# Scan outputs of two head groups per visit to TensorE's column halves, broadcast rows in one run, and two prices in the planner

## The chip, the cores and the metric

The kernel runs on one core of one Trainium2 chip. The metric is the device time of one execution in microseconds (us), the median of several runs. TensorE is PE in the profile (its weight loads are PEld), VectorE is DVE, ScalarE is ACT, GpSimd is POOL, and SP is the engine whose queue issues almost all transfers.

## The reference, cut to what matters

One layer of a hybrid model works on 128 prompt tokens and 2048 latent tokens. Eight heads of differential attention and sixteen heads of a two-directional state-space scan share one input projection and one output projection. The scan runs in 17 chunks of 128 tokens. For each chunk and head, the part that the change touches is

```
seg    = a_cum[q] - a_cum[s]
Lmat   = exp(where(mask, seg, -inf))
cb     = C[q] . B[s]                       # shared by the 4 heads of a group
y_diag = (cb * Lmat) @ (x * dt)            # 128 x 128 by 128 x 64 for each head
y_off  = (C @ h_prev) * exp(a_cum)         # h_prev: state at the chunk's edge, 64 x 64
y      = y_diag + y_off                    # both directions are summed
```

The sixteen heads lie in four groups (g) of four heads. The prompt chunk (chunk 0) starts from a state of zero and has no `y_off`.

## The kernel before, in words

The whole program is recorded first and ordered afterwards. `body` calls operations on a `Plan`; each call becomes an `Op` with a price (`price`), the operations that it depends on, and a function that emits the real instruction. `latest` walks the recorded order backwards and gives each operation a due time, with TensorE's operations due in the order in which they were recorded. `simulate` then plays the program forward on the prices, one operation per engine at a time, and among those that are ready takes the one that is due first. A DMA occupies a modelled wire for its price. What comes out is the order of every engine's queue and of SP's DMA queue; on the chip each queue runs strictly in that order. All instructions are emitted by one helper, so that the profile shows one line (L233) for all of them.

The change is in the stage of the scan outputs (`ssd_outputs`). It runs beside the projection units of q, k, g and z: `run_units` puts one or two steps of the scan (`pipe(k)`) between the matmuls of a projection unit (24 matmuls in three products of hi and lo parts, PSUM tile `ps_p`) and that unit's eviction. `G` lists the 68 pairs of chunk and head group, from chunk 16 down to chunk 0. For pair j:

- `loads(j)`, at step j, issues the transfers on SP's queue. `ar` receives the decay rows of a group, two directions by four heads by 128 tokens, broadcast to all 128 partitions from `row_d` (512 KB written). For g = 0 it also loads `bz`, `cd`, `hb` (the states, from `hb_d`) and `xs`.
- `stage_a1(j)`, at step j + 2: ACT takes exponentials of the rows into `ea` and DVE multiplies them by `cd`; POOL masks `ar`, ACT takes eight more exponentials, and PE forms `ps_cb` (fp32, 128 columns of weights). For g = 0 DVE first updates `hb` by way of `hd`, and so waits for the load of `hb`.
- `stage_a2(j)`, the same step: DVE adds the two directions into `ms` and multiplies by `ps_cb`.
- `stage_m(j)`, at step j + 3: PE forms the outputs of four heads. Each matmul has 64 columns of weights and writes one half of the PSUM partitions, so two heads run side by side in the column halves of the array. For two pairs of heads and two terms (`xs` by `ms`, then `hb` by `ea`) these are eight matmuls in fp32, each of which the trace shows as two records: 16 records on `ps_y`. Chunk 0 has the first term only, 8 records.
- `stage_e(j)`: ACT copies `ps_y` (128x256) to `y`, and a DMA stores it to `y_d`.

`ms` has two buffers, `ea` and `ar` three, the PSUM tag `y` two banks. The rows in `row_d` are written by `dt_rows`, earlier, from transposes of `a_all`, in the order chunk, direction, head, token: the four heads of a group are 2 KB in one run, and a group's two directions lie 8 KB apart.

In `price` a DMA costs by its innermost run, up to 4096 bytes; for the broadcast of `ar` that is 256 runs of 2 KB, 1.35 us of the modelled wire. A matmul with 64 columns of weights has a price of its own, but going from full columns to column halves and back costs nothing in `simulate`.

Of the kernel before, what the change touches and what calls it, by code (L numbers as in the profile page):

```python
# [18 lines left out]
P = 128  # L19
# [148 lines left out]
class Op:  # L168
    __slots__ = ("i", "eng", "emit", "cost", "deps", "weak", "outs", "then", "n", "late", "due", "start", "end", "tab", "port")

# [25 lines left out]
class Plan:  # L196


    def __init__(self, tc):
        self.tc, self.ops, self.last, self.floor, self.line, self.lean = tc, [], None, None, None, False  # L200
        for k in ("tensor", "vector", "scalar", "gpsimd", "sync"):
            setattr(self, k, Engine(self, k))
# [13 lines left out]
    def add(self, eng, name, args, kw):  # L216
# [13 lines left out]
        def emit():  # L230
# [3 lines left out]

        op = Op(i, eng, emit, self.price(eng, name, named))
        f = str(named.get("func", "")).rsplit(".", 1)[-1]
        op.tab = TABLE.get(f)
        inside = sum(isinstance(v, View) and not v.t.pool.psum and math.prod(v.shape[1:]) > 1
                     for k, v in named.items() if k not in ("out", "accum_out"))
# [4 lines left out]
        if self.line is not None and eng == "dma":  # L244
            op.weak.update(self.line)
            self.line[:] = [i]
        self.ops.append(op)
        for v in reads + writes:
# [17 lines left out]
        op.weak.discard(i)  # L266
        op.weak -= op.deps

    def touch(self, op, v, write):
# [20 lines left out]
    def price(self, eng, name, a):  # L290
# [3 lines left out]
        if eng == "dma":  # L294
            named_in = a["in_"]
            run = min(4096, 4 * min(o.shape[-1], named_in.shape[-1]))
            return max(math.prod(o.shape) * 4 / run * max(9.7 + 0.0365 * run, 28.4) / 16, 180.0) if run > 4 else 180.0
        n = max([size(o)] + [size(v) for v in ins[:1]])
# [72 lines left out]
    def simulate(self):  # L371
# [4 lines left out]
        free = dict.fromkeys(ENG, 0.0)  # L376
        wire, table, port = 0.0, None, 0.0
        pend = {e: [] for e in ENG}
# [28 lines left out]
        while True:  # L407
# [21 lines left out]
            if be == "dma":  # L429
                wire = max(wire, bt + 700) + op.cost  # L430
                end = wire + 1100
                free[be] = max(bt + 480, wire - 1500)
            else:
                c = op.cost
                if op.tab and op.tab != table:
                    c += 1283
                    table = op.tab
                if op.port:
                    c += max(port - bt, 0.0)
                    port = bt + c  # L440
                free[be] = end = bt + c
# [6 lines left out]
def body(tc, I, O):  # L448
# [17 lines left out]
    xt_d = dp.tile([NCH, P, D], F32, name="xt_d")  # L466
    row_d = dp.tile([NCH, 2, 16, P], F32, name="row_d")
    hb_d = dp.tile([NCH, P, D], F32, name="hb_d")
# [481 lines left out]
    def dt_chain():  # L950
        t_a, t_b, t_c = (vc.tile([P, NCH, 32], F32, name=n, tag=n) for n in ("t_a", "t_b", "t_c"))
        dts["t"] = (t_a, t_b)
        nc.vector.tensor_scalar(out=t_a, in0=dt_all, scalar1=-1.0, scalar2=None, op0=ALU.mult)
# [15 lines left out]
    def dt_sums():  # L969
        t_a, t_b = dts["t"]  # L970
        for d, tri in enumerate((triu, tril)):
            sl = slice(d * 16, d * 16 + 16)
            pc = bank("tr")
            mm(pc[:, :272], lhsT=tri, rhs=t_a[:, :, sl], start=True, stop=True)
            nc.vector.tensor_copy(out=a_all[:, :, sl], in_=pc[:, :272].rearrange("p (c h) -> p c h", h=16))
            po = bank("y")
            mm(po[:, :272], lhsT=ones, rhs=t_a[:, :, sl], start=True, stop=True)
            nc.vector.tensor_copy(out=t_b[:, :, sl], in_=po[:, :272].rearrange("p (c h) -> p c h", h=16))
        nc.scalar.activation(out=dec_all, in_=t_b, func=AF.Exp)
        nc.vector.tensor_tensor(out=t_b, in0=t_b, in1=a_all, op=ALU.subtract)  # L980
        nc.scalar.activation(out=t_b, in_=t_b, func=AF.Exp)
        nc.vector.tensor_tensor(out=w_all, in0=t_b, in1=dt_all, op=ALU.mult)
        nc.vector.tensor_scalar(out=dt_all, in0=dt_all, scalar1=TINY, scalar2=None, op0=ALU.max)
        nc.scalar.activation(out=dt_all, in_=dt_all, func=AF.Ln)
        nc.vector.tensor_tensor(out=dt_all, in0=dt_all, in1=a_all, op=ALU.subtract)

    def dt_rows(c0):
        k = min(4, NCH - c0)
        pr = bank("tr")
        for i in range(k):  # L990
            nc.tensor.transpose(pr[:32, i * P:(i + 1) * P], a_all[:, c0 + i, :], ident)
        rw = vc.tile([32, 512], F32, tag="rw", name="rw", bufs=2)
        nc.vector.tensor_copy(out=rw[:, :k * P], in_=pr[:32, :k * P])
        store(out=row_d[c0:c0 + k].rearrange("c d h t -> (d h) c t"),
              in_=rw[:, :k * P].rearrange("r (c t) -> r c t", t=P))
# [106 lines left out]
    def ssd_outputs(sp):  # L1102
# [9 lines left out]
        def loads(j):  # L1112
# [3 lines left out]
            if g == 0:  # L1116
# [9 lines left out]
                if c:  # L1126
# [4 lines left out]
            ar = sp.tile([P, 2, 4, P], F32, tag="ar", name="ar", bufs=3)  # L1131
            load(out=ar.rearrange("p d h t -> p d (h t)"),
                 in_=row_d[c, :, g * 4:g * 4 + 4, :].rearrange("d h t -> d (h t)").unsqueeze(0).to_broadcast(
                     [P, 2, 512]))
            w[0], w[1] = ar[:, 0], ar[:, 1]

        def stage_a1(j):
# [8 lines left out]
            if c:  # L1146
                ea = w["es"] = sp.tile([P, 4, P], F32, tag="ea", name="ea", bufs=3)
                nc.scalar.activation(out=ea[0:64], in_=w[0][0:64], func=AF.Exp)
# [12 lines left out]
        def stage_a2(j):  # L1161
            w = W[j]
            ms = w["ms"] = sp.tile([P, 4, P], F32, tag="ms", name="ms", bufs=2)
            nc.vector.tensor_tensor(out=ms, in0=w[0], in1=w[1], op=ALU.add)
# [3 lines left out]
        def stage_m(j):  # L1168

            c, g = G[j]  # L1170
            w, k = W[j], CK[c]
            py = w["py"] = bank("y")
            for i in range(2):
                o = py[:, i * P:(i + 1) * P]
                for n, (st, mv) in enumerate((("xs", "ms"), ("hb", "es"))[:2 if c else 1]):
                    for e in range(2):
                        cs = slice((g * 4 + 2 * i + e) * 64, (g * 4 + 2 * i + e + 1) * 64)
                        mm(o[e * 64:e * 64 + 64], lhsT=k[st][:, cs], rhs=w[mv][:, 2 * i + e],
                           start=n == 0, stop=n == 1 or not c)

        def stage_e(j):
            c, g = G[j]
            w = W.pop(j)
            y = sp.tile([P, 2, P], F32, tag="y", name="y", bufs=2)
            nc.scalar.copy(out=y, in_=w["py"][:, :256].rearrange("p (i t) -> p i t", t=P))
            store(out=y_d[2 * g:2 * g + 2, :, c * P:(c + 1) * P].rearrange("i p t -> p i t"), in_=y)

        def pipe(k):
            n = len(G)
            if k == 0:  # L1190
                init()
            if 0 <= k - 3 < n:
                stage_m(k - 3)
            if 0 <= k - 2 < n:
                stage_a1(k - 2)
            if 0 <= k - 3 < n:
                stage_e(k - 3)
# [651 lines left out]
```

## Time and profile before

| what | value |
|---|---|
| median of 3 runs | 3131.48 us (3130.55 to 3132.58) |
| the profiled execution, its own time | 3144.34 us |
| its span, first to last instruction | 3142.6 us |
| mean granted TensorE clock | 0.992 |
| PE busy over the span | 3073.5 us (98%) |
| chain that ended last, share of PE | 78%; DMA 10%, DVE 8% |

The page's second part cuts the span into 40 slices; PE is at nine tenths or more in all but the first. The stage of the scan outputs lies from about 846 to 1432 us. A record's duration is not the time that it costs, since matmuls are pipelined: what an instruction costs PE is read from the distance between starts. An engine's "idle before" names what ended the wait, which may be an engine or a transfer.

### The profile page before, as it was taken

How to read it: one execution, taken by the hardware profiler on the slowest of the kernel's cores; microseconds unless marked ns; L12 is line 12 of the kernel's file. 1: busy time of each engine (PE TensorE's matmuls, PEld its weight loads, DVE VectorE, ACT ScalarE, POOL GpSimd, SP SyncE). 2: the span in 40 equal slices, each digit the busy share in tenths (PEclk: the TensorE clock that was granted, in tenths of full speed). 3: DMA queues.
4: the chain of work that ended last, by engine and by line, in shares of the span. 5: the costliest groups of instructions: out<-in, count | busy, mean ns of one | idle time of the engine just before them, and what ended most of it. 6: DMA issues, size and time to landing. Idle time of an engine off the chain costs nothing.

```text
span 3142.6 us, 56037 instructions
## 1 busy us (share of the span) xinstructions
PE 3073.5 (98%) x20539; PEld 2900.9 (92%) x20539; DVE 2309.5 (73%) x4636; ACT 1835.9 (58%) x3290; POOL 1327.3 (42%) x1171
## 2 busy tenths in 40 slices
PE   7999999999999999999999999999999999999999
PEld 5999999988999998898999999999999999878887
DVE  5544524767675776664699999999999999877775
ACT  3233312333465676663588888888888888754432
POOL 2010100000021122220499999999999999800000
PEclk9999999999999999999999999999999999999999
DMA  8633322677788788879313131222222221296663
GB/s 282 214 120 102 125 80 96 200 234 227 215 254 238 224 228 210 224 198 224 89 41 95 35 96 50 80 67 68 65 67 65 66 64 46 82 275 195 182 189 106
DMA packets 490725, 449.27 MB, mean 143 GB/s; under 512 B 34991, under 2 KB 437704, under 8 KB 490450
## 3 DMA queue, kind: packets, MB, share of 16 engines
q1 hardware_dynamic: 488530, 445.52, 48.8%
q8 instruction: 162, 2.65, 0.4%
q14 instruction: 113, 0.93, 0.1%
q10 hardware_dynamic: 1920, 0.17, 0.0%
HBM read 305.96 MB, written 139.62 MB: 142 GB/s over the span
## 4 chain that ended last, share of the span: by engine, by line
PE 78%; DMA 10%; DVE 8%; issue 2%; SPq 1%; ACT 1%; POOL 0%; DVEq 0%; POOLq 0%; ACTq 0%
PE ps_p L233 28%; PE ps_s L233 17%; PE ps_o L233 13%; PE ps_t L233 8%; PE ps_v L233 4%; PE ps_y L233 3%; PE ps_f L233 3%; DMA yL<-y_d 2%; SPq L233 1%; DVE o L233 1%; DVE yx L233 1%; PE ps_tr L233 1%; PE ps_cb L233 1%; DMA hb<-hb_d 1%; DMA vr<-in_w_in 1%
## 5 line engine op out<-in xcount | busy, mean ns | idle before, releaser
L233 DVE TENSOR_SCALAR_CACHE_REDUCE S<-ps_s 128x768 f32<-128x768 f32 x768 | 726.4, 953 | 65.3 <-PE ps_s L233 50.3
L233 POOL TENSOR_TENSOR S<-S,S 128x768 f32<-128x768 f32 x384 | 708.0, 1866 | 5.0
L233 PE MATMUL ps_s<-K,q 128*128 128x384 f32 x3072 | 707.6, 348 | 0.4 <-DVE S L233 0.3
L233 PE MATMUL ps_p<-hH,wH 128*128 128x384 f32 (+1 forms) x2112 | 699.6, 331 | 0.0
L233 PE MATMUL ps_p<-hH,wL 128*128 128x384 f32 (+1 forms) x2112 | 691.4, 327 | 0.4 <-DVE wL L233 0.4
L233 PE MATMUL ps_p<-hL,wH 128*128 128x384 f32 (+1 forms) x2112 | 691.4, 327 | 0.0
L233 ACT ACTIVATE S<-S,mx 128x2304 f32<-128x2304 f32 x256 | 570.9, 2230 | 12.9 <-DVE mx L233 12.9
L233 PEld LDWEIGHTS ps_s<-K,q 128*128 128x128 f32 x3072 | 505.8, 189 | 2.6 <-DVE S L233 2.1
L233 PE MATMUL ps_o<-aH,V 128*128 128x256 f32 x2304 | 490.9, 286 | 0.0
L233 POOL TENSOR_SCALAR_AFFINE_SELECT ar<-ar 128x512 f32<-128x512 f32 x136 | 113.4, 839 | 746.9 <-ACT ea L233 686.6
L233 ACT CAST aH<-ps_t 128x384 fp32r<-128x384 f32 x768 | 347.7, 481 | 133.5 <-PE ps_t L233 130.1
L233 DVE TENSOR_TENSOR aL<-ps_t,aH 128x384 fp32r<-128x384 f32 x768 | 406.1, 550 | 25.7 <-ACT aH L233 21.7
L233 PEld LDWEIGHTS ps_p<-hH,wL 128*128 128x128 f32 x2112 | 399.2, 189 | 1.7 <-DVE wL L233 1.1
L233 PEld LDWEIGHTS ps_p<-hH,wH 128*128 128x128 f32 x2112 | 399.6, 189 | 1.1 <-issue 0.6
L233 PEld LDWEIGHTS ps_p<-hL,wH 128*128 128x128 f32 x2112 | 399.9, 189 | 0.4 <-issue 0.2
L233 POOL TENSOR_SCALAR S<-S,sm 128x768 f32<-128x768 f32 x384 | 346.4, 916 | 91.9 <-DVE sm L233 82.0
L233 PEld LDWEIGHTS ps_o<-aH,V 128*128 128x128 f32 x2304 | 380.9, 189 | 0.1
L233 PE MATMUL ps_t<-cst,S 128*128 128x128 f32 x2304 | 355.9, 272 | 1.3 <-DVE aL L233 1.3
L233 PE MATMUL ps_o<-aL,V 128*128 128x256 f32 x1152 | 330.0, 286 | 0.0
L233 PEld LDWEIGHTS ps_t<-cst,S 128*128 128x128 f32 x2304 | 285.3, 140 | 16.4 <-DVE aL L233 1.5
L233 DVE TENSOR_TENSOR wL<-wr,wH 128x1024 fp32r<-128x1024 f32 x88 | 110.9, 1260 | 191.8 <-ACT wH L233 188.5
L233 PEld LDWEIGHTS ps_o<-aL,V 128*128 128x128 f32 x1152 | 218.2, 189 | 0.5 <-DVE mx L233 0.3
(245 smaller groups left out, 4737.0 us busy)
## 6 DMA issues: line engine op xcount, KB each, us to landing
wr<-in_w_in SPq DMA_DIRECT2D x88, 512.0 KB
ar<-row_d SPq DMA_DIRECT2D x68, 512.0 KB
q<-qH_d SPq DMA_DIRECT2D x128, 128.0 KB
q<-qL_d SPq DMA_DIRECT2D x128, 128.0 KB
xb<-xbc_d SPq DMA_DIRECT2D x17, 640.0 KB
K<-kH_d SPq DMA_DIRECT2D x48, 192.0 KB
K<-kL_d SPq DMA_DIRECT2D x48, 192.0 KB
V<-vH_d SPq DMA_DIRECT2D x24, 384.0 KB
```

Of the source, the lines that this page charges most:

```text
L233: getattr(e, name)(*[rl(v) for v in args], **{k: rl(v) for k, v in kw.items()})
```

## The change

1. `stage_m` is called for every second pair and covers two head groups: it forms the outputs of pairs j - 1 and j in one PSUM bank (four blocks of 128 columns in place of two). The new `Plan.together` records all its matmuls as one operation, so that they stay in one piece. `pipe` calls `stage_m` and `stage_e` at even steps only. `stage_e` copies 128x512 at once and stores four rows of tiles in one DMA. `ms` gets four buffers and `ea` five.
2. `row_d` is laid out by chunk, group, direction, head, token, so that a group's rows are one run of 4 KB; the broadcast reads `[P, 1024]` from one run. For this `dt_sums` makes two more DVE copies (into `t_c`, in the new order), and `dt_rows` transposes `t_c`.
3. The planner charges 95 ns whenever TensorE goes between matmuls with 64 columns of weights and anything else, and prices a broadcast of `row_d` at 300 ns for each 4 KB over 16 engines, 2.4 us.

```diff
+        if self.one:
+            op = self.ops[self.one[0]]
+            op.emit = lambda a=op.emit: (a(), emit())
+            op.cost += self.price(eng, name, named)
+            i = op.i
+        else:
+            op = Op(i, eng, emit, self.price(eng, name, named))
+            self.ops.append(op)
+        if self.one is not None:
+            self.one[:] = [i]
...
+        op.half = name == "matmul" and named["lhsT"].shape[-1] == 64
...
+    def together(self, f):
+
+        self.one = []
+        f()
+        self.one = None
...
+            if isinstance(named_in, View) and named_in.t.kw["name"] == "row_d":
+                return math.prod(o.shape) * 4 / 4096 * 300.0 / 16
...
+                if be == "tensor" and op.half != half:
+                    c += 95
+                    half = op.half
...
-    row_d = dp.tile([NCH, 2, 16, P], F32, name="row_d")
+    row_d = dp.tile([NCH, 4, 8 * P], F32, name="row_d")
...
+            nc.vector.tensor_copy(out=t_c.rearrange("p c (g d h) -> p c g d h", g=4, d=2)[:, :, :, d],
+                                  in_=a_all[:, :, sl].rearrange("p c (g h) -> p c g h", g=4))
...
-            nc.tensor.transpose(pr[:32, i * P:(i + 1) * P], a_all[:, c0 + i, :], ident)
+            nc.tensor.transpose(pr[:32, i * P:(i + 1) * P], t_c[:, c0 + i, :], ident)
...
-            load(out=ar.rearrange("p d h t -> p d (h t)"),
-                 in_=row_d[c, :, g * 4:g * 4 + 4, :].rearrange("d h t -> d (h t)").unsqueeze(0).to_broadcast(
-                     [P, 2, 512]))
+            load(out=ar.rearrange("p d h t -> p (d h t)"), in_=row_d[c, g].unsqueeze(0).to_broadcast([P, 1024]))
...
-                ea = w["es"] = sp.tile([P, 4, P], F32, tag="ea", name="ea", bufs=3)
+                ea = w["es"] = sp.tile([P, 4, P], F32, tag="ea", name="ea", bufs=5)
...
-            ms = w["ms"] = sp.tile([P, 4, P], F32, tag="ms", name="ms", bufs=2)
+            ms = w["ms"] = sp.tile([P, 4, P], F32, tag="ms", name="ms", bufs=4)
...
         def stage_m(j):
 
-            c, g = G[j]
-            w, k = W[j], CK[c]
-            py = w["py"] = bank("y")
-            for i in range(2):
-                o = py[:, i * P:(i + 1) * P]
-                for n, (st, mv) in enumerate((("xs", "ms"), ("hb", "es"))[:2 if c else 1]):
-                    for e in range(2):
-                        cs = slice((g * 4 + 2 * i + e) * 64, (g * 4 + 2 * i + e + 1) * 64)
-                        mm(o[e * 64:e * 64 + 64], lhsT=k[st][:, cs], rhs=w[mv][:, 2 * i + e],
-                           start=n == 0, stop=n == 1 or not c)
+            py = W[j]["py"] = bank("y")
+
+            def run():
+                for j2 in (j - 1, j):
+                    c, g = G[j2]
+                    w, k = W[j2], CK[c]
+                    for i in range(2):
+                        o = py[:, (g % 2 * 2 + i) * P:(g % 2 * 2 + i + 1) * P]
+                        for n, (st, mv) in enumerate((("xs", "ms"), ("hb", "es"))[:2 if c else 1]):
+                            for e in range(2):
+                                cs = slice((g * 4 + 2 * i + e) * 64, (g * 4 + 2 * i + e + 1) * 64)
+                                mm(o[e * 64:e * 64 + 64], lhsT=k[st][:, cs], rhs=w[mv][:, 2 * i + e],
+                                   start=n == 0, stop=n == 1 or not c)
+            pl.together(run)
 
         def stage_e(j):
             c, g = G[j]
+            del W[j - 1]
             w = W.pop(j)
-            y = sp.tile([P, 2, P], F32, tag="y", name="y", bufs=2)
-            nc.scalar.copy(out=y, in_=w["py"][:, :256].rearrange("p (i t) -> p i t", t=P))
-            store(out=y_d[2 * g:2 * g + 2, :, c * P:(c + 1) * P].rearrange("i p t -> p i t"), in_=y)
+            y = sp.tile([P, 4, P], F32, tag="y", name="y", bufs=2)
+            nc.scalar.copy(out=y, in_=w["py"].rearrange("p (i t) -> p i t", t=P))
+            store(out=y_d[2 * g - 2:2 * g + 2, :, c * P:(c + 1) * P].rearrange("i p t -> p i t"), in_=y)
 
         def pipe(k):
             n = len(G)
             if k == 0:
                 init()
-            if 0 <= k - 3 < n:
+            full = 0 <= k - 3 < n and k % 2 == 0
+            if full:
                 stage_m(k - 3)
             if 0 <= k - 2 < n:
                 stage_a1(k - 2)
-            if 0 <= k - 3 < n:
+            if full:
                 stage_e(k - 3)
             if 0 <= k - 2 < n:
                 stage_a2(k - 2)
```

## Rows read from the trace of the kernel before

**Rows 1.** The page, its first part: busy time of each engine, its share of the span and its instructions.

```profile
PE 3073.5 (98%) x20539; PEld 2900.9 (92%) x20539; DVE 2309.5 (73%) x4636; ACT 1835.9 (58%) x3290; POOL 1327.3 (42%) x1171
```

**Rows 2.** Stretches of the span, for the stage of the scan outputs (from the first broadcast to the last visit). Columns: the stretch, its length, busy us (and instructions) of PE, PEld, DVE, ACT and POOL, then the granted TensorE clock as a share of full speed, the busy share of the 16 DMA engines, and GB/s.

```profile
846.00:1432.00 586.00, 573.02 (x4008) 543.45 (x4007) 405.55 (x710) 370.59 (x926) 113.42 (x136) 0.99 0.81 223
```

**Rows 3.** Instructions of PE in order of time around one full visit to the column halves. Columns: start, duration, engine, line, operation and tiles, shape, and how many were merged into the row.

```profile
871.12 0.33 PE L233 MATMUL ps_p<-hL,wH 128*128 128x384 f32 x1
871.30 0.34 PE L233 MATMUL ps_p<-hH,wL 128*128 128x384 f32 x1
871.57 0.44 PE L233 MATMUL ps_y<-ms,xs 128*64 128x128 f32 x4
871.84 0.39 PE L233 MATMUL ps_y<-ea,hb 128*64 128x128 f32 x4
872.05 0.39 PE L233 MATMUL ps_y<-ms,xs 128*64 128x128 f32 x4
872.27 0.39 PE L233 MATMUL ps_y<-ea,hb 128*64 128x128 f32 x4
872.59 0.49 PE L233 MATMUL ps_cb<-cd,bz 128*128 128x128 f32 x2
872.83 0.42 PE L233 MATMUL ps_p<-hH,wH 128*128 128x384 f32 x1
873.09 0.33 PE L233 MATMUL ps_p<-hL,wH 128*128 128x384 f32 x1
```

**Rows 4.** The same view around the last visit of the stage. It belongs to chunk 0, which has no state term, so it holds half as many matmuls, and a projection follows it directly.

```profile
1430.09 0.34 PE L233 MATMUL ps_p<-hH,wL 128*128 128x384 f32 x1
1430.36 0.66 PE L233 MATMUL ps_y<-ms,xs 128*64 128x128 f32 x8
1430.95 0.44 PE L233 MATMUL ps_p<-hH,wH 128*128 128x384 f32 x1
1431.23 0.34 PE L233 MATMUL ps_p<-hL,wH 128*128 128x384 f32 x1
```

**Rows 5.** The same view around a product of B and C (`ps_cb`) that stands alone among projections, with no visit ahead of it.

```profile
864.04 0.34 PE L233 MATMUL ps_p<-hH,wL 128*128 128x384 f32 x1
864.21 0.38 PE L233 MATMUL ps_cb<-cd,bz 128*128 128x128 f32 x2
864.35 0.36 PE L233 MATMUL ps_p<-hH,wH 128*128 128x256 f32 x1
864.55 0.28 PE L233 MATMUL ps_p<-hL,wH 128*128 128x256 f32 x1
864.67 0.28 PE L233 MATMUL ps_p<-hH,wL 128*128 128x256 f32 x1
```

**Rows 6.** The instructions that read or write the PSUM tile `ps_y`: counts, and durations in ns (minimum/median/maximum), first and last start in us.

```profile
L233 PE MATMUL ps_y<-ms,xs x544: 272/273/421, 871.6 to 1430.7; 128*64 128x128 f32 x182
L233 ACT COPY y<-ps_y x68: 345/373/380, 876.0 to 1431.2; 128x256 f32<-128x256 f32 x68
L233 ACT COPY s_b<-ps_y x36: 579/581/584, 642.5 to 842.1; 64x512 f32<-64x512 f32 x36
```

**Rows 7.** Who waited for whom in the stretch 846 to 1440 us, on PE, DVE and the DMA queue of SP: total us, times, longest.

```profile
PE ps_tr L233 <- DVE kl L233: 8.5, 2, 7.1
PE ps_y L233 <- DVE ms L233: 4.1, 1, 4.1
DVE hb L233 <- DMA hb<-hb_d: 46.8, 10, 11.7
SPq L233 <- DMA ar<-row_d: 19.4, 17, 3.1
```

**Rows 8.** Instructions in order of time on the DMA queue of SP and on DVE ahead of the two longest stalls of the stage. In brackets: idle time of the engine before the instruction, and what ended it.

```profile
1212.00 0.38 SPq L233 DMA_DIRECT2D z_d<-so  x1
1215.58 0.37 SPq L233 DMA_DIRECT2D y_d<-y  x1
1216.04 0.42 SPq L233 DMA_DIRECT2D ar<-row_d  x1
1216.55 0.46 SPq L233 DMA_DIRECT2D hb<-hb_d  x1
1224.72 1.22 DVE L233 TENSOR_TENSOR hb<-hb,hd 64x1024 f32<-64x1024 f32 x1 [7.89 <-DMA hb<-hb_d]
1323.35 1.22 DVE L233 TENSOR_TENSOR hb<-hb,hd 64x1024 f32<-64x1024 f32 x1 [11.70 <-DMA hb<-hb_d]
```

**Rows 9.** Stretches as in rows 2: the two stalls of PE, each with the stretch behind it.

```profile
1220.40:1227.50 7.10, 0.04 (x1) 0.00 (x0) 2.71 (x3) 0.00 (x0) 0.00 (x0) 0.76 0.60 202
1227.50:1231.00 3.50, 3.42 (x12) 3.42 (x13) 3.47 (x11) 3.34 (x10) 1.27 (x2) 0.52 0.46 105
1321.80:1326.00 4.20, 0.14 (x1) 0.00 (x0) 2.62 (x4) 0.00 (x0) 0.00 (x0) 1.00 0.27 96
1326.00:1330.00 4.00, 3.96 (x25) 3.66 (x26) 3.66 (x9) 2.03 (x6) 0.70 (x2) 0.57 0.71 127
```

**Rows 10.** Stretches as in rows 2: first one in which almost only a broadcast of `row_d` into `ar` is under way (two runs of 2 KB for each of 128 partitions), then one with a broadcast of `rs_d` into `rb` alone (one run of 4 KB for each of 128 partitions, the same 512 KB; output projection).

```profile
976.70:980.60 3.90, 3.90 (x29) 3.73 (x26) 3.80 (x7) 2.26 (x4) 0.64 (x1) 1.00 0.81 169
2849.50:2851.60 2.10, 2.10 (x11) 1.74 (x10) 2.10 (x4) 0.72 (x2) 0.00 (x0) 1.00 0.80 244
```

**Rows 11.** One instruction of DVE in order of time: a copy of 128x272 out of PSUM in `dt_sums`.

```profile
603.84 0.42 DVE L233 COPY t_b<-ps_y 128x272 f32<-128x272 f32 x1
```

More of the change, by code (lines that the diff above doesn't have):

```diff
@@ L168 @@
 class Op:
-    __slots__ = ("i", "eng", "emit", "cost", "deps", "weak", "outs", "then", "n", "late", "due", "start", "end", "tab", "port")
+    __slots__ = ("i", "eng", "emit", "cost", "deps", "weak", "outs", "then", "n", "late", "due", "start", "end", "tab", "port", "half")
     def __init__(self, i, eng, emit, cost):
@@ L199, in __init__ @@
     def __init__(self, tc):
-        self.tc, self.ops, self.last, self.floor, self.line, self.lean = tc, [], None, None, None, False
+        self.tc, self.ops, self.last, self.floor, self.line, self.lean, self.one = tc, [], None, None, None, False, None
         for k in ("tensor", "vector", "scalar", "gpsimd", "sync"):
@@ L246, in add @@
             self.line[:] = [i]
-        self.ops.append(op)
         for v in reads + writes:
@@ L376, in simulate @@
         free = dict.fromkeys(ENG, 0.0)
-        wire, table, port = 0.0, None, 0.0
+        wire, table, port, half = 0.0, None, 0.0, False
         pend = {e: [] for e in ENG}
@@ L951, in dt_chain @@
         t_a, t_b, t_c = (vc.tile([P, NCH, 32], F32, name=n, tag=n) for n in ("t_a", "t_b", "t_c"))
-        dts["t"] = (t_a, t_b)
+        dts["t"] = (t_a, t_b, t_c)
         nc.vector.tensor_scalar(out=t_a, in0=dt_all, scalar1=-1.0, scalar2=None, op0=ALU.mult)
@@ L969, in dt_sums @@
     def dt_sums():
-        t_a, t_b = dts["t"]
+        t_a, t_b, t_c = dts["t"]
         for d, tri in enumerate((triu, tril)):
@@ L987, in dt_rows @@
     def dt_rows(c0):
+        t_c = dts["t"][2]
         k = min(4, NCH - c0)
@@ L990, in dt_rows @@
         for i in range(k):
-            nc.tensor.transpose(pr[:32, i * P:(i + 1) * P], a_all[:, c0 + i, :], ident)
+            nc.tensor.transpose(pr[:32, i * P:(i + 1) * P], t_c[:, c0 + i, :], ident)
         rw = vc.tile([32, 512], F32, tag="rw", name="rw", bufs=2)
         nc.vector.tensor_copy(out=rw[:, :k * P], in_=pr[:32, :k * P])
-        store(out=row_d[c0:c0 + k].rearrange("c d h t -> (d h) c t"),
+        store(out=row_d[c0:c0 + k].rearrange("c g (e t) -> (g e) c t", t=P),
               in_=rw[:, :k * P].rearrange("r (c t) -> r c t", t=P))
```

1 line of the change is left out of this document (removed).

## The prediction

> **What bounds the kernel now.** I read the busy parts of the page first: PE is busy for 98% of the span, the next engine, DVE, for 73% [rows 1]. Then the stretch of the scan outputs alone: of 586 us PE is busy 573, DVE 406, ACT 371, POOL 113, and the 16 DMA engines 81% [rows 2]. So in this stage, too, PE sets the end, DMA is the one resource that comes near, and DVE, ACT and POOL have a third of their time free. Two things shorten it: fewer nanoseconds of PE per visit, and fewer stalls. Work that only leaves ACT, DVE or SP's queue is worth nothing by itself. Idle PE is 13 us of the 586; the list of waits puts 8.5 us on DVE's `kl` and 4.1 us on DVE's `ms` [rows 7].
>
> **What a visit costs, and what the change removes.** Durations of PE's records overlap, so I use distances between starts. In the visit at 871.57 us, from the last projection matmul before it (871.30) to the second one after it (873.09) pass 1.79 us [rows 3]. What should that stretch hold at a steady rate? A projection matmul of 384 columns takes 0.17 (from 864.04 to 864.21 [rows 5]; from 871.12 to 871.30 in the rounded rows of [rows 3]). A block of four `ps_y` records inside the visit takes 0.43 / 2 = 0.215 (871.84 to 872.27 [rows 3]); there are four. For the two records of `ps_cb`, the one that stands alone gives 864.04 to 864.55 = 0.51 for itself, a 384-column and a 256-column matmul; less 0.17 and 0.12 (864.55 to 864.67) that is 0.22 [rows 5]. Sum: 0.17 + 4 x 0.215 + 0.22 + 0.17 = 1.42. The excess is 0.37 us.
>
> Is the excess per visit, or per matmul? The visit at 1430.36 has 8 records and no `ps_cb` behind it: 1430.09 to 1431.23 = 1.14 us against 0.17 + 2 x 0.215 + 0.17 = 0.77, an excess of 0.37 again [rows 4]. So it comes once per visit, whether it is long or short and whatever follows. It lies at the edges: about 0.1 between the last full matmul and the first half one, the slow first block (0.27 to the next block instead of 0.215), about 0.1 on the way out, and about 0.1 in the first full weights after it. The trace shows 544 `ms` records, 8 for each of 68 visits, and 68 copies of `ps_y` [rows 6]. The change makes 34 visits, by construction: the recorded unit can't be torn apart. 34 x 0.36 (a little under the excess, for rounded starts) = 12.2 us, all on PE's path. The bounds are 10 (0.30, if part of the edge is a wait that a longer visit keeps) and 13.
>
> Which steps could take some of that back? The 34 `ps_cb` that no longer follow a visit stand alone, and a lone one costs no more than its own work [rows 5]: nothing. The matmuls themselves are the same in number and shape.
>
> **What leaves the other engines.** 68 ACT copies of 368 to 373 ns become 34 of 128x512, for which the copies of 64x512 out of the same tile, 581 ns, are the nearest row [rows 6]: 25.4 - 19.8 = 5.6 us of ACT that is not the bound. 34 stores to `y_d` leave SP's queue, with 0.37 us of issue each [rows 8]. Both count as nothing; they only make other commands earlier.
>
> **What is added.** Two DVE copies in `dt_sums`; the nearest row is a 128x272 copy, 0.42 us [rows 11], so 0.84 us in all. They come before the transposes of `dt_rows`, while PE has projection units to do: 0 if these cover it, 0.8 if not; I take 0. A visit now holds PE for about 1.9 us in one piece, and the eviction of the projection ahead of it does not depend on it: 0. The visit waits for the `ms` and `ea` of two pairs instead of one. The first is a step older than before. The second is as fresh as before. Behind the waiting instruction stand the next projection units on PE, and behind those the evictions on ACT and DVE. With the pair's lead unchanged I take 0; the bound is in the rivals.
>
> **The broadcast and the stalls.** Why did PE stand still for 7.1 us at 1220 and 4.1 us at 1322 [rows 7, 9]? In both places DVE stood at its update of `hb`, waiting for the load (7.9 and 11.7 us idle, [rows 8]), and the `kl` or `ms` that PE needed was queued behind that update on DVE. The load was late for two reasons. SP's queue stood between `z_d` at 1212.0 and `y_d` at 1215.6 [rows 8]; the list of SP's waits has 19.4 us, 17 times, on the landing of an `ar` broadcast, the longest 3.1 us [rows 7]. And `hb` was issued right behind the next broadcast [rows 8]. A broadcast in two runs of 2 KB kept the DMA engines busy for about 0.81 x 3.9 = 3.2 us, of which 169 GB/s x 3.9 = 659 KB leaves 135 KB to others; by share of bytes about 2.5 us. The kernel also has a broadcast in one 4 KB run, `rb`: 0.80 x 2.1 = 1.7 us for 244 x 2.1 = 512 KB [rows 10]. So the new form should hand over about 1.7 us sooner (3.9 against 2.1 us of stretch, rounded), and the planner, which had 1.35 us for it, will have 2.4 and will not put `hb`'s update ahead of work that PE needs as eagerly.
>
> The stalls have a tail. Behind each the granted clock is 0.52 and 0.57, between the levels of 1.2 and 2.4 GHz and near the lower, for 3.5 and 4.0 us [rows 9]: lost (1 - 0.52) x 3.5 = 1.7 and (1 - 0.57) x 4.0 = 1.7. Together the stalls cost 7.1 + 1.7 + 4.1 + 1.7 = 14.6 us. What goes? At the first, 3.1 of queue and 1.7 of broadcast; at the second, 1.7: 6.5 us, with the rest left late next (the update itself, 1.2 us on DVE, and the `hd` behind it). The ends are 14.6 (both go) and some microseconds below nothing (a new order of all queues can make a stall elsewhere). The profiled execution is 12.9 us longer than the median, so part of what it shows as stalls may not be in the timed runs. I take 4.
>
> One rule speaks against this term: the Trainium skill, "DMA: Bandwidth & Descriptors", section Specifications, holds that 512 B per transfer are enough for full rate; by it runs of 2 KB gain nothing from becoming 4 KB, and the sum would be the visits alone. The rows differ, 1.7 against some 2.5 us [rows 10]; with other traffic in the first of them, that is not settled.
>
> **The rivals.**
> 1. *The visits alone.* The broadcast is no faster in this place, or the new order trades the old stalls for new ones: -12.2 us, plus 0 to 6 for one more stall like the second (4.1 + 1.7). About 3120, between 3118 and 3126. For it: the stalls are few, so that one accident decides. Against it: [rows 10]. The DMA page's rule, if it holds, gives this case.
> 2. *More stalls go.* Both stalls in full, 14.6, with the visits 12.2: 3131.5 - 26.8 = 3105; some smaller ones could go too. For it: SP's queue is lighter, and both have one cause. Against it: what is left of the lateness after 1.7 to 4.8 us.
> 3. *Slower: PE waits at the long visits.* A visit can't start before both pairs' `ms` are there, and is not split around a late one. The trace has one such wait, 4.1 us and 1.7 us of slow clock, at a visit whose DVE work stood behind `hb` [rows 7, 9]. If the planner, with visits as blocks and a dearer broadcast, puts DVE's `ms` closer to the visits, two more waits of 5.8 us eat the gain, and at four the kernel is slower: 4 x 5.8 - 12.2 = +11, 3142. It decides from one wait in eight or so of the 34 visits. Against it: of 68 visits one waited, and DVE has a third of its time free [rows 2].
> 4. *It doesn't do what it says.* If the matmuls of a visit were split by others, or the excess came back in the middle (new weights for another pair), the visits would give nothing: 3127 with the stall term. Against it: inside a visit the step from `ms` to `ea` and to the next pair of heads costs nothing extra [rows 3]. Small.
>
> **How the numbers follow.** Profiled span 3142.6 - 12.2 - 4.0 + 0 = 3126.4; the same 16.2 us off the median 3131.5 give 3115.3, so 3115 us. Chances: forecast (3109 to 3119) 0.47, the visits alone 0.24, more stalls gone 0.14, slower 0.10, not what it says 0.05. This kernel's measurement can tell about 0.2% from no change, 6.3 us, so "faster" is below 3125.2 and "slower" above 3137.7. Faster: 0.47 + 0.14 + 0.11 from the visits alone, where no more than one short stall comes in = 0.72. Slower 0.09; the rest, 0.19, is within. For 8 in 10 the range runs from 3099 (rival 2 with the smaller stalls) to 3132 (the visits' gain eaten by two new stalls); outside are the slower case and an extreme of the second rival.
>
> **What would show it.** Right: 34 copies of `ps_y` of about 0.58 us; 32 records in a full visit with one excess of 0.36; PE's busy time in the stage down by some 12 us; a broadcast that lands about 2 us sooner; less of "SP waits for `ar`" and of "DVE `hb` waits for `hb_d`". Wrong: an excess in the middle of a visit; idle PE ahead of `ps_y` on DVE's `ms`, several times; packets of `ar` as slow as before; or a change outside the stage as large as that inside it.

## The result, and the profile after

The changed kernel takes 3108.47 us (median of 4 runs, 3107.31 to 3110.31) against 3131.02 us (4 runs, 3129.33 to 3132.58) for the kernel before on the same chip: ratio 0.9929, 95% interval 0.9911 to 0.9946, 22.5 us less. The profiled execution takes 3110.31 us, its span 3108.4. The prediction had 3115, and 3099 to 3132 for 8 in 10.

The page of the changed kernel, its first part, and the chain that ended last by engine:

```profile
PE 3053.4 (98%) x20539; PEld 2899.3 (93%) x20539; DVE 2298.6 (74%) x4638; ACT 1833.1 (59%) x3256; POOL 1330.3 (43%) x1171
...
PE 90%; DMA 5%; DVE 2%; ACT 1%; SPq 1%; issue 1%; POOL 0%; DVEq 0%; POOLq 0%; ACTq 0%
```

PE has the same number of instructions as in [rows 1] and is busy 20 us less. Of the chain DMA and DVE had 18% and have 7%. That is a share of the path that was followed back, not of time that PE lost: idle PE over the whole span falls from 69.1 to 55.0 us.

The stage of the scan outputs, as a stretch with the columns of [rows 2]:

```profile
846.00:1432.00 586.00, 585.52 (x4184) 570.77 (x4183) 408.84 (x721) 378.58 (x907) 112.45 (x136) 1.00 0.75 235
```

Of the 13.0 us in which PE stood still in [rows 2], half a microsecond is left (the stage ends earlier now, so the last 27 us of the stretch lie behind it); the clock is 1.00, and the DMA engines are busy 75% instead of 81% while they move more bytes in a second.

Waits in 846 to 1440 us, to be read beside [rows 7]:

```profile
PE ps_p L233 <- DVE wL L233: 0.3, 1, 0.3
PE ps_cb L233 <- DVE ysm L233: 0.2, 1, 0.2
...
DVE hb L233 <- DMA hb<-hb_d: 24.4, 9, 7.9
...
SPq L233 <- DMA ar<-row_d: 1.0, 2, 0.8
```

PE's waits on `kl` and `ms` (12.6 us) are gone, and SP's on `ar` are down from 19.4 to 1.0 (a second profile of the kernel before has 14.8). DVE still waits 24 us for the load of `hb`, in one place as long as 7.9 us, and PE does not notice: not the wait costs time, but what is queued behind it.

One visit of the changed kernel, PE in order of time, as in [rows 3]:

```profile
1043.52 0.33 PE L233 MATMUL ps_p<-hL,wH 128*128 128x384 f32 x1
1043.69 0.34 PE L233 MATMUL ps_p<-hH,wL 128*128 128x384 f32 x1
1043.96 0.44 PE L233 MATMUL ps_y<-ms,xs 128*64 128x128 f32 x4
1044.23 0.39 PE L233 MATMUL ps_y<-ea,hb 128*64 128x128 f32 x4
1044.45 0.39 PE L233 MATMUL ps_y<-ms,xs 128*64 128x128 f32 x4
1044.66 0.39 PE L233 MATMUL ps_y<-ea,hb 128*64 128x128 f32 x4
1044.88 0.39 PE L233 MATMUL ps_y<-ms,xs 128*64 128x128 f32 x4
1045.10 0.39 PE L233 MATMUL ps_y<-ea,hb 128*64 128x128 f32 x4
1045.32 0.39 PE L233 MATMUL ps_y<-ms,xs 128*64 128x128 f32 x4
1045.54 0.39 PE L233 MATMUL ps_y<-ea,hb 128*64 128x128 f32 x4
1045.86 0.49 PE L233 MATMUL ps_cb<-cd,bz 128*128 128x128 f32 x2
1046.10 0.42 PE L233 MATMUL ps_p<-hH,wH 128*128 128x384 f32 x1
1046.36 0.33 PE L233 MATMUL ps_p<-hL,wH 128*128 128x384 f32 x1
```

Eight blocks of four records stand in one piece, with 0.22 us from each to the next after the first. From 1043.69 to 1046.36 pass 2.67 us; at a steady rate it would be 0.17 + 8 x 0.215 + 0.22 + 0.17 = 2.28, an excess of 0.39 for the pair of groups. It comes once, as before [rows 3], and nothing is lost where the second group begins.

How long is the stage, free of its place in the span? I take the distance from the last record of `ps_y<-xw` (the stage before) to the last of `ps_y<-ms`. Both are last starts in the view by tile. In the changed kernel:

```profile
L233 PE MATMUL ps_y<-xw,bd x272: 379/379/431, 643.9 to 844.4; 128*64 128x256 f32 x136
...
L233 PE MATMUL ps_y<-ms,xs x544: 272/273/324, 881.7 to 1404.4; 128*64 128x128 f32 x182
L233 ACT COPY y<-ps_y x34: 565/588/592, 884.9 to 1404.8; 128x512 f32<-128x512 f32 x34
```

1404.4 - 844.4 = 560.0 us, where the kernel before has 589.0 in the profile of the rows above and 586.6 in a second one (experiment 1). The last row has the 34 copies of 0.588 us.

### The profile page after: what moved, and what is told of

Read it like the earlier page. It is cut to its first block, busy times and chain, and to the rows that moved or that the text cites. A ratio compares the mean times of both kernels' runs of the same rounds, so it can differ in the third digit from the quotient of the medians.

```text
span 3108.4 us, 55817 instructions
## 1 busy us (share of the span) xinstructions
PE 3053.4 (98%) x20539; PEld 2899.3 (93%) x20539; DVE 2298.6 (74%) x4638; ACT 1833.1 (59%) x3256; POOL 1330.3 (43%) x1171
## 4 chain that ended last, share of the span: by engine, by line
PE 90%; DMA 5%; DVE 2%; ACT 1%; SPq 1%; issue 1%; POOL 0%; DVEq 0%; POOLq 0%; ACTq 0%
PE ps_p L233 31%; PE ps_s L233 17%; PE ps_o L233 13%; PE ps_f L233 11%; PE ps_t L233 8%; PE ps_v L233 5%; PE ps_y L233 4%; PE ps_tr L233 1%; PE ps_cb L233 1%; SPq L233 1%; DMA wraw<-in_w_out 1%; DMA wm<-in_w_mod 1%; DMA vL_d<-vL 0%; DMA qL_d<-cc 0%; DVE S L233 0%
```

## The experiments

The question is how the 26.6 us (586.6 - 560.0) divide among long visits, rows and prices, and why the stalls went. Theory C lays that to transport: the broadcast in one run is faster, so SP's queue and the load of `hb` are. Theory D lays it to the order: the planner, with a truer price, puts DVE's work elsewhere. The table has for each kernel the ratio to the kernel before on the same chip, the length of the stage as just defined, idle PE in 846 to 1432 us (586 less PE's busy time) and DVE's wait for the load of `hb` there. The last two columns divide the stage itself: slow clock is the sum, over stretches of 0.5 us, of PE's busy time times what the granted clock lacks to 1.00, and the last column is the stage less its own idle PE and less that. All but the median and the ratio come from one profiled execution each, which can lie some 4 us from the median of its kernel; the runs were on several chips, on which the kernel before has medians of 3131 to 3136 us, so kernels are compared by ratio or by the distance from the kernel before on their chip.

| kernel | median us | ratio (95%) | stage | idle PE | DVE waits for hb_d | slow clock | rest of the stage |
|---|---|---|---|---|---|---|---|
| before, run again | 3134.76 | 0.9995 (0.9986 to 1.0005) | 586.6 | 11.0 | 44.0 | 3.3 | 572.4 |
| visits alone | 3126.50 | 0.9966 (0.9951 to 0.9980) | 581.9 | 13.7 | 45.0 | 7.3 | 560.9 |
| rows alone | 3130.19 | 0.9981 (0.9971 to 0.9990) | 576.8 | 3.0 | 25.8 | 1.5 | 572.3 |
| broadcast's price alone | 3126.80 | 0.9971 (0.9960 to 0.9983) | 580.3 | 5.6 | 31.5 | 2.5 | 572.2 |
| rows and broadcast's price | 3121.33 | 0.9961 (0.9946 to 0.9976) | 571.9 | 0.0 | 9.9 | 0.0 | 571.9 |
| changed, rows as before | 3120.66 | 0.9958 (0.9942 to 0.9974) | 573.4 | 9.5 | 41.2 | 1.7 | 562.7 |
| changed, without prices | 3116.56 | 0.9950 (0.9933 to 0.9966) | 564.8 | 4.7 | 24.2 | 0.0 | 560.2 |
| changed | 3108.47 | 0.9929 (0.9911 to 0.9946) | 560.0 | 0.5 | 24.4 | 0.0 | 559.8 |
| visits of four groups | 3109.85 | 0.9926 (0.9910 to 0.9943) | 560.6 | 4.8 | 26.6 | 1.7 | 554.1 |
| before, hb planned later | 3115.41 | 0.9946 (0.9933 to 0.9958) | 571.9 | 0.3 | 3.9 | 0.0 | 571.9 |
| changed, rows as before, hb planned later | 3111.80 | 0.9932 (0.9919 to 0.9944) | 565.3 | 3.9 | 2.2 | 1.5 | 560.2 |
| four groups, hb planned later | 3106.58 | 0.9920 (0.9907 to 0.9934) | 558.9 | 4.6 | none listed | 0.0 | 554.3 |
| the same, five buffers | 3100.02 | 0.9897 (0.9884 to 0.9911) | 559.6 | 4.0 | none listed | 1.5 | 554.1 |

The last column goes almost entirely by the number of visits. With 68 it is 571.9 to 572.4 us, with 17 it is 554.1 to 554.3, and with 34 it is 559.8 to 560.9 in four kernels and 562.7 in a fifth. That one has nine short waits of PE, and of each some 0.16 us are not counted as idle, since a matmul's record lasts 0.33 us where the next one could start after 0.17; that is 1.4 of its surplus of 2.4 us.

**1. The kernel before, run again.** No edit.

> The kernel before, unchanged, for a second profile. The stalls of PE in the scan outputs (7.1 us ahead of a transpose of kl, 4.1 us ahead of ps_y) are a property of the order of the queues, by the prediction's theory: then they stand at the same instructions again, with lengths that differ by a few us, and the time is 3131 us within 0.1%. By the rival, that they were accidents of the one profiled execution (whose span was 11 us above the median), they are gone or stand elsewhere.

Its span is 3129.9 us, 12.7 less than that of the profile that the prediction read, and the stalls stand at the same instructions: PE waits 6.3 us on `kl` (longest 5.4) and 4.6 on `ms`, against 8.5 and 4.1 in [rows 7]. They belong to the order of the queues and not to one execution. The median, 3134.76, is a little more than 0.1% over 3131, but the kernel before has 3136.0 on this chip. Behind the two stalls the clock is slow as in [rows 9]:

```profile
1218.50:1222.50 4.00, 4.00 (x16) 4.00 (x17) 3.70 (x10) 3.89 (x12) 1.27 (x2) 0.61 0.43 120
1317.40:1321.50 4.10, 4.10 (x26) 3.77 (x27) 3.76 (x9) 2.24 (x6) 0.91 (x2) 0.61 0.54 147
```

The 12.7 us lay elsewhere: 5.8 before the transposes of `dt_rows` (first start 595.3 against 601.1 us), 0.5 from there to the first `xw`, 2.4 in the stage and 4.0 behind it.

**2 to 4. Each part alone.**

```diff
 visits_only, against the kernel before: together, stage_m, stage_e, pipe, ms and ea as in the change; no other line
 rows_only: row_d, dt_sums, dt_rows and the load of ar as in the change; no other line
 bprice_only:
+            if isinstance(named_in, View) and named_in.t.kw["name"] == "row_d":
+                return math.prod(o.shape) * 4 / 4096 * 300.0 / 16
```

> The kernel before with the merged visits alone (stage_m and stage_e over two groups, together, the deeper ms and ea), old rows, no new price. Theory A (0.36 us per visit, on PE's path): 34 visits fewer, 12.2 us, so 3119 us, plus or minus 6 for stalls that the new order makes or removes; a full visit of 32 records shows one excess of 0.36 us and no second one in its middle. Theory B (the gain of 22 us came from the new order, and the edges of a visit were cover for something else): 3131 us. SP's waits for ar stay near 19 us by either.

> The kernel before with the new layout of row_d alone (one run of 4 KB, the two copies in dt_sums), 68 visits, the planner without the two new prices (its old formula then gives 1.27 us instead of 1.35 for a broadcast). Theory C (the stalls come from how slowly the broadcast is carried): a broadcast takes 1.7 us of the 16 DMA engines instead of 2.5, SP's waits for ar fall from 19 us to a few, the wait of DVE for hb to half, and the time is 3131 - 6.5 = 3124 us. Theory D (they come from the order that too low a price gives): SP's waits and the stalls stay about the same, 3131 us within 5.

> The kernel before with the planner's price of the broadcast alone (2.4 us), old rows, 68 visits, no price for mode changes. Theory D (order): the stalls of 7.1 and 4.1 us shrink or go, 3131 - 10 = 3121 us, although each broadcast is as slow as before. Theory C (transport): SP's waits for ar stay near 19 us, stalls of the same size stand somewhere, 3131 us within 5.

The visits alone lower the median by 9.5 us on their chip, within what theory A allows (12.2, plus or minus 6). In the profiled execution, the slowest of the five, the stage is shorter by 4.7 us only: its last column falls by 11.5, and stalls of their own take the rest back, on PE:

```profile
PE ps_tr L233 <- DVE kl L233: 7.7, 3, 3.8
PE ps_cb L233 <- DVE ms L233: 4.5, 2, 4.1
PE ps_y L233 <- DVE ms L233: 1.2, 1, 1.2
```

Behind them the granted clock is 0.50 for 4.3 us (and 0.80 for 4.2 more), 0.61 for 4.2 and 0.50 for 4.7: 2.2 + 0.8 + 1.6 + 2.4 = 7 us of slow clock on top of 13.7 us of idle PE. The rows alone take away 8.0 of the 11.0 us of idle PE, with theory C's signs: SP waits 3.3 us on `ar`, DVE's wait for `hb` falls by some 40%, and the median is 5.8 us lower (6.5 forecast). With the price alone SP still waits 20.2 us on `ar`, and yet 5.4 of the 11.0 us go, and the median is 9.2 us lower (10 by theory D). So neither theory is enough by itself.

What the rows do to the transport is plain on the page, DMA queue 1 (packets, MB, share of 16 engines), first of the kernel before run again, then with the new rows alone:

```profile
q1 hardware_dynamic: 488530, 445.52, 48.5%
```

```profile
q1 hardware_dynamic: 479826, 445.52, 47.1%
```

The same bytes go in 8704 = 68 x 128 packets fewer, and the engines are busy 0.485 x 3129.9 - 0.471 x 3126.1 = 45.6 us less, 0.67 us for each broadcast. (The changed kernel against its version with the old rows gives 56.7 us in the same way, 0.83 each.) One kernel differs by as much as 15.6 us from profile to profile: the two of the kernel before have 1533.6 and 1518.0. But the two groups keep apart: seven profiles with the old rows have 1508 to 1534 us, seven with the new 1458 to 1478. Between the means lie 50 us, 0.73 for each broadcast.

**5. Rows and broadcast's price, visits as before.** The lines of 3 and 4 together.

> 68 visits as before, with the new layout of the rows and the broadcast's new price, without the price of mode changes. Theory A (three terms that add: 34 edges at 0.36 us are worth 12 us by themselves, and the stalls go by rows and price): idle PE in the stage of the scan outputs 3 us or less, no slow clock behind it; from the last xw record to the last visit 572 us (560 of the changed kernel + 12), 3119 to 3122 us in all. Theory B (the stalls are a matter of the visits' order as much; without the long visits some stay): idle PE in the stage 5 us or more, 576 us or more, 3125 us or more.

The stage, as a stretch:

```profile
846.00:1432.00 586.00, 586.00 (x4107) 557.89 (x4106) 413.34 (x717) 380.49 (x935) 114.83 (x136) 1.00 0.75 230
```

No idle PE, clock 1.00, 571.9 us. The changed kernel has none to speak of either and takes 560.0: the 34 visits fewer are worth 11.9 us, 0.35 each. That is theory A, which had 572. The changed kernel has the price of mode changes and more buffers as well, but with no idle time on either side these can't tell in the stage, and the last column of the table gives the same: 12 us from 68 visits to 34, 6 us from 34 to 17, 0.35 us for each visit both times.

**6 and 7. The changed kernel without one of its parts.** First with the old layout of the rows, then without the two prices.

```diff
 after_oldrows
-            load(out=ar.rearrange("p d h t -> p (d h t)"), in_=row_d[c, g].unsqueeze(0).to_broadcast([P, 1024]))
+            load(out=ar.rearrange("p d h t -> p d (h t)"),
+                 in_=row_d[c, :, g * 4:g * 4 + 4, :].rearrange("d h t -> d (h t)").unsqueeze(0).to_broadcast(
+                     [P, 2, 512]))
...
 after_noprices
-            if isinstance(named_in, View) and named_in.t.kw["name"] == "row_d":
-                return math.prod(o.shape) * 4 / 4096 * 300.0 / 16
...
-                if be == "tensor" and op.half != half:
-                    c += 95
-                    half = op.half
```

> The changed kernel with the rows laid out as before (two runs of 2 KB for each broadcast, no t_c copies), merged visits and both prices kept. Theory C (the transport's speed is what took the stalls away): SP's queue still waits some 19 us for ar, idle PE in the stage 6 us or more, 3115 us or more. Theory D (what counts is that the planner knows what a broadcast takes; the 2 KB runs are slow but early enough): SP's waits on ar stay near 19 us, yet idle PE in the stage is 3 us or less, and without the stall of some 2.5 us near 620 us that came with the rows the time is 3105 to 3111 us.

> The changed kernel without both prices: merged visits and rows in one run. Theory C (transport): SP's waits on ar 5 us or less, idle PE in the stage 4 us or less, 3109 to 3113 us. Theory D (price): four or so stalls in the stage as with the visits alone, idle PE 8 us or more, 3118 us or more.

With long visits the price does not do it alone: 9.5 us of idle PE, in pieces, and a stage 13.4 us longer than the changed kernel's. Without the prices 4.7 us of idle PE come back, 4.8 us of stage; these 4.7 and the median of 3116.56 lie between what C and D have, and meet neither. In the stage the rows are worth more than the prices here, as theory C has it; the medians of the two runs have intervals that overlap. And a number of both expectations for the old rows was wrong: SP's wait on `ar` with the old rows is 8.5 us, not some 19, and stalls are there all the same:

```profile
SPq L233 <- DMA ar<-row_d: 8.5, 8, 2.3
...
DVE hb L233 <- DMA hb<-hb_d: 41.2, 11, 8.8
...
PE ps_tr L233 <- DVE kl L233: 4.2, 3, 2.2
PE ps_cb L233 <- DVE ms L233: 2.1, 2, 1.1
PE ps_y L233 <- DVE ms L233: 1.1, 1, 1.1
```

SP's wait does not go with the stalls. DVE's wait for `hb` is long wherever stalls are, though the changed kernel has 24.4 us of it without them. That gave theory H: the planner takes the load of `hb` to land sooner than it does, so it puts the update of `hb` on DVE ahead of work that PE needs; rows and price helped by way of it. By its code the planner has the load land 0.7 + 1.3 + 1.1 = 3.1 us after its issue, somewhat later behind a broadcast; at the stall shown under experiment 9, 8.1 us pass from the issue to the update that waits for it.

**8. Visits of four groups.** One visit for a chunk, in two PSUM banks.

```diff
-            py = W[j]["py"] = bank("y")
+            py = W[j]["py"] = [bank("y"), bank("y")]
...
-                for j2 in (j - 1, j):
+                for j2 in range(j - 3, j + 1):
...
-            full = 0 <= k - 3 < n and k % 2 == 0
+            full = 0 <= k - 3 < n and k % 4 == 2
```

> A dose more: the changed kernel with one visit for a whole chunk (four groups, two PSUM banks, 17 visits; ms has six buffers and ea eight). Theory A (one excess of 0.36 us for each visit, whatever its length): 17 edges fewer are worth 6 us, 3102 us, PE's idle time in the stage as in the changed kernel. Rival (the visits' length has a price: four pairs' ms and ea have to be ready at once, and the projection's evictions wait behind 3.3 us of PE in one piece): waits of PE on ms or new idle time of 6 us or more in the stage, 3108 us or more.

No gain: three waits on `kl`, 4.8 us, and 1.7 us of slow clock eat what the 17 edges give (554.1 against 559.8 us in the last column). The time is in the rival's range, the idle PE under its 6 us, and none of it is on `ms`.

**9 to 12. The load of hb, planned to land 4 us later.** One edit to the planner, on three kernels; no operation of the program is added or taken away. It does two things at once: the load is due 4 us earlier, and so may be issued earlier, and what needs it is planned for 4 us later. The two were not run apart. The fourth has a fifth buffer for three tiles as well.

```diff
+        op.far = 4000.0 if eng == "dma" and isinstance(named["in_"], View) and named["in_"].t.kw.get("name") == "hb_d" else 0.0
...
-                t -= 2000.0 if op.eng == "dma" else 0.0
+                t -= 2000.0 + op.far if op.eng == "dma" else 0.0
...
-                end = wire + 1100
+                end = wire + 1100 + op.far
...
 quad_hb_cc5 too (also for kl and cc)
-                so = pb.tile([P, 384], F32, tag="cc", name="so", bufs=4)
+                so = pb.tile([P, 384], F32, tag="cc", name="so", bufs=5)
```

> The kernel before with one thing changed: the planner takes the load of the states (hb from hb_d) to land 4 us later than it did and to be due 4 us earlier; layout of the rows, visits and prices as before. Theory H (the stalls have one cause: DVE stands at the update of hb because that load lands late, and the rows' transport and price helped by way of it): DVE's wait on hb_d falls from 44 to 47 us to 20 us or less, idle PE in the stage from 11 to 13 us to 4 us or less, 3116 to 3122 us. Rival R (the slow broadcasts themselves hold up SP's queue and PE's feeders, hb or not): idle PE in the stage 7 us or more, 3126 us or more.

> The changed kernel with the rows laid out as before (2 KB runs) and the same 4 us of lead for the load of hb. Theory H: the 9.0 us of idle PE that the old rows left in the stage fall to 3 us or less, 3106 to 3112 us, so that the new layout is not needed. Rival R: 6 us or more stay, 3116 us or more.

> The visits of four groups with the same 4 us of lead for the load of hb. Theory H: the three waits on kl behind the update of hb (4.8 us of idle PE and some 2 us of slow clock) go; with the 6 us of the 17 edges that is 3102 to 3104 us. Rival (the waits come with visits of 3.3 us in one piece): idle PE in the stage 4 us or more, 3108 us or more.

> The same with a fifth buffer for the tiles so, kl and cc that hold outputs of the projection until they are stored, against the wait of ACT on a store near 620 us. If that stall is one of buffers it goes (1 to 2 us less than without, if it is there at all); if it is one of SP's queue or of the order, nothing changes.

The first is the clearest run of the study. Old rows, old prices, 68 short visits: 3115.41 us, 17.2 below the kernel before on its chip (H had 3116 to 3122), and the stage has the 571.9 us of experiment 5, with no idle PE in it. How does it look at the first stall? First the kernel before run again, SP's queue and DVE:

```profile
1206.94 0.42 SPq L233 DMA_DIRECT2D ar<-row_d  x1
1207.46 0.46 SPq L233 DMA_DIRECT2D hb<-hb_d  x1
...
1215.54 1.22 DVE L233 TENSOR_TENSOR hb<-hb,hd 64x1024 f32<-64x1024 f32 x1 [6.18 <-DMA hb<-hb_d]
1216.80 1.22 DVE L233 TENSOR_TENSOR hd<-hb,dec_all 64x1024 f32<-64x1024 f32 x1
1218.05 0.29 DVE L233 COPY kl<-ps_p 128x128 f32<-128x128 f32 x1
```

Then with `hb` planned later:

```profile
1204.72 0.67 SPq L233 DMA_DIRECT2D hb<-hb_d  x1
1207.80 0.37 SPq L233 DMA_DIRECT2D ar<-row_d  x1
...
1212.58 0.29 DVE L233 COPY kl<-ps_p 128x128 f32<-128x128 f32 x1 [2.03 <-DMA ar<-row_d]
1213.82 1.22 DVE L233 TENSOR_TENSOR hb<-hb,hd 64x1024 f32<-64x1024 f32 x1 [0.94 <-DMA hb<-hb_d]
```

The load goes out 2.7 us earlier, although the stage began 2.6 us later in this execution, and ahead of the broadcast instead of behind it. The copy of `kl`, for which PE's transposes wait, stands ahead of the update. The load itself is no quicker: 9.1 us pass from its issue to the update, 8.1 before. And SP waits as long for `ar` as before the edit (19.4 and 14.8 us in the two profiles of the kernel before):

```profile
SPq L233 <- DMA ar<-row_d: 19.0, 19, 2.4
...
DVE hb L233 <- DMA hb<-hb_d: 3.9, 3, 2.5
```

At the second stall the load still follows a broadcast, and there the `ms` that PE needs stands ahead of the update (1302.19 against 1306.15 us; in the kernel before run again 1315.90 against 1314.64). So theory H holds for the kernel before, and the slow broadcast does no harm once load and update are planned like this. With long visits and old rows it holds in the main: the median is that of the changed kernel (ratio 0.9932 against 0.9929), within H's 3106 to 3112, but 3.9 us of idle PE stay where H allowed 3. With visits of four groups H is not met: 3106.58 us lies between the two sides, and 4.6 us of idle PE stay, which is the rival's sign (4 or more), although DVE no longer waits for `hb`. So stalls here have another cause as well. In the last kernel, around its longest stall:

```profile
POOL ar L233 <- ACT ea L233: 10.2, 2, 7.0
DVE ea L233 <- ACT ea L233: 4.3, 1, 4.3
ACT ea L233 <- DMA ar<-row_d: 3.8, 1, 3.8
...
PE ps_tr L233 <- DVE kl L233: 2.6, 1, 2.6
```

Here it is the broadcast that lands late, ACT's exponentials wait for it, DVE for these, and `kl` stands behind. This was not tried further. Free of idle time and of the 1.5 us of slow clock behind that stall (0.65 for 4.4 us) its stage is 559.6 - 4.0 - 1.5 = 554.1, against 559.8: 5.7 us for 17 edges, 0.33 each. Over all kernels of the table it is 0.35: the edge has one price whatever the visit's length, as theory A has it. The edit was not run on the changed kernel as it is, with the new rows and visits of two groups.

The fifth buffer was to remove a stall that all kernels with the new rows and four buffers have near 620 us. In the changed kernel, 600 to 640 us:

```profile
PE ps_p L233 <- ACT so L233: 2.9, 1, 2.9
...
ACT so L233 <- DMA qL_d<-cc: 3.2, 1, 3.2
```

ACT may not overwrite a `cc` buffer until its store has landed. With five buffers the list of PE's waits there holds 0.2 us, and from the first transpose of `dt_rows` to the first `xw` pass 38.0 us (597.1 to 635.1) against 41.9 with four (600.7 to 642.6): 3.9 us, twice what was expected. The median falls by 6.6; the rest lies ahead of the transposes, where executions of one kernel differ by as much (experiment 1), and stays unexplained. This kernel, 3100.02 us, is the fastest of the study: 1% below the kernel before; its interval touches that of the changed kernel at 0.9911.

## Why the prediction came out as it did

- *The visits.* Predicted 34 x 0.36 = 12.2 us; measured 11.9, between two kernels without stalls. The excess is one for each visit, none appears in the middle, and the sum leaves no room for a cost of the lone `ps_cb`. The step stands.
- *The stalls: the step that was mis-sized.* I took 4 us of 14.6. In the stage 26.6 us went: 12.6 in the last column of the table, 10.7 of idle PE (11.0 to 0.3 within the stage) and 3.3 of slow clock behind the stalls. So 14.0 went where 4 were forecast; the upper end, the second rival, was the case. Both reasons for the discount fell: the second execution, 12.7 us shorter, has the same stalls; and nothing was "left late next", because the update of `hb` changed its place on DVE and not only its time. At the place of the first stall the changed kernel has

```profile
1204.49 0.44 SPq L233 DMA_DIRECT2D ar<-row_d  x1
...
1205.52 0.44 SPq L233 DMA_DIRECT2D hb<-hb_d  x1
...
1212.32 0.29 DVE L233 COPY kl<-ps_p 128x128 f32<-128x128 f32 x1 [0.25 <-PE ps_p L233]
...
1214.99 1.22 DVE L233 TENSOR_TENSOR hb<-hb,hd 64x1024 f32<-64x1024 f32 x1
```

  The load still goes out behind a broadcast, and 9.5 us pass until the update, but `kl` stands ahead of it. That the time came within 7 us of the forecast is in part luck: 10 us more of stalls went, and a part of that came back outside the stage.
- *The cause of the stalls* was half right. DVE's wait for `hb` with PE's work queued behind it was read correctly from [rows 7, 8]. But I put its lateness down to SP's queue (3.1 us) and the broadcast (1.7), and experiment 9 removes the stalls while SP waits as long as before and each broadcast is as slow. What counts is where the planner puts the load and the update; whether the earlier issue or the later place of the update does more there is open. As I read it, a faster broadcast is one way to bring the landing to where the planner has it, a higher price another, and a later landing in the plan the direct one.
- *The broadcast's gain.* I had 2.5 against 1.7 us of all DMA engines, 0.8 less; measured 0.73, between the means of seven profiles each. How much sooner a single broadcast lands (about 2 us by the prediction) was not measured. The rule that spoke against it (the Trainium skill, "DMA: Bandwidth & Descriptors", section Specifications) does not hold in this place: from runs of 2 KB to 4 KB, far over its 512 B, the same bytes took some 50 us less of the DMA engines.
- *The copies in `dt_sums`.* Taken as 0, with a bound of 0.8: wrong in kind. From the first transpose of `dt_rows` to the first `xw` the changed kernel takes 41.6 us (602.3 to 643.9), the kernel before 39.5 (595.3 to 634.8): 2.1 lost to a stall that neither copy's duration shows. Seven profiles with the old rows have 39.5 to 40.1 us there, the six with the new rows and four buffers 41.6 to 43.7. I had the queues' movement in view for the stage alone. Whether the copies, the new form of the stores or the new order as a whole brings the stall was not separated.
- *PE waits at long visits*, the slower case, did not come true. The visits alone do bring 13.7 us of idle PE, but only 1.2 of them ahead of `ps_y` on `ms`; the others stand at `kl` and `ps_cb`. In the whole change they are gone. Which of the two prices gives the 4.8 us of experiment 7 stays open.

The sum for the two profiles: -26.6 in the stage, +2.1 at `dt_rows`, +7.0 ahead of it (602.3 against 595.3), -3.9 behind the stage; -21.4 of span, as 3129.9 to 3108.4 within rounding. The +7.0 differs between executions and is no effect of the change that I could show: the first transpose of `dt_rows` starts at 595.3 to 601.1 us in the seven profiles with the old rows, at 597.1 to 602.3 in the seven with the new.

## What to carry to other kernels

Where a planner fixes the order of strict queues, its idea of when a transfer lands can be worth more than the transfer's speed: find the consumer that waits for a load, ask what of the engine that sets the end is queued behind it, and try first to correct the landing in the plan. Count the edges between modes by the distance of starts, and measure what fewer of them bring between two kernels without stalls, since new stalls can hide it. And follow an edit through the queues of its own stage too: a new form of the rows, priced at two copies of 0.4 us, came with a stall of 2.9 us some 20 us later.

## What the hardware showed that I had not expected

The DMA engines are sensitive to the run of a broadcast between 2 KB and 4 KB: 68 broadcasts of 512 KB cost 0.73 us more of all 16 engines, each, in runs of 2 KB than in runs of 4 KB (means of seven profiles each). And a wait of PE of one length does not always have the same tail. In the two kernels with visits of four groups and `hb` planned later, with four buffers and then with five, PE waits 2.64 us at the same transpose:

```profile
1104.13 0.33 PE L233 MATMUL ps_tr<-cst,kl 128*128 128x128 f32 x1 [2.64 <-DVE kl L233]
```

```profile
1096.71 0.47 PE L233 MATMUL ps_tr<-cst,kl 128*128 128x128 f32 x1 [2.64 <-DVE kl L233]
```

Behind the first the granted clock is 1.00, behind the second 0.65 for 4.4 us. What decides between the two no run here shows.
